# Whole-buffer weight splits, 1024-column loads and row-indexed token DMAs in a two-block transformer forward pass

## The chip, the cores and the metric

The kernel runs on one core of one Trainium2 chip. The metric is device time in microseconds of one execution. Before the change the median of three runs is 2467.13 us (2462.75 to 2468.89).

## What is computed

The input is x, 256 tokens of width 1024 in float32. A first block has two layers of four sequence mixers (their branches gated and merged) and a feed-forward part; that part is dense in layer 0 and a mixture of eight experts, two per token, in layer 1. A second block of two layers (latent attention, pooling, a spatial gate, a convolution, and a feed-forward part) follows. The change concerns the mixture of experts, and the way in which every weight is prepared.

```python
def swiglu(h, w1, w3, w2):
    return (jax.nn.silu(h @ w1) * (h @ w3)) @ w2

def moe_ffn(h, router_w, w1, w3, w2):            # h [1, 256, 1024]; w1, w3 [8, 1024, 2816]; w2 [8, 2816, 1024]
    logits = (h @ router_w).astype(jnp.float32)
    top_vals, top_idx = lax.top_k(logits, TOP_K)  # TOP_K = 2
    top_w = jax.nn.softmax(top_vals, axis=-1)
    gate = jnp.sum(jax.nn.one_hot(top_idx, N_EXPERTS) * top_w[..., None], axis=-2)
    out = jnp.zeros_like(h)
    for e in range(N_EXPERTS):
        out = out + gate[..., e:e + 1] * swiglu(h, w1[e], w3[e], w2[e])
    return out
```

## The kernel before

**Weights.** All weights come from DRAM in float32, in buffers of 128 partitions by 1024 columns (`raw`, and `rawp` for buffers that are halves of a larger tile; six everywhere, twenty in the experts). `wload` (L171) splits each into two parts in TensorE's format `fp32r` whose sum is the weight: ScalarE casts it (L190, `whi`), and VectorE or GpSimd subtracts (L191, `wlo` = `raw` - `whi`). It does so in pieces of at most 512 columns, two a buffer, with ten pairs of piece buffers (`SPBUFS`). Every seventh piece in the experts (`POOLN`), every third elsewhere (`POOLD`), is subtracted on GpSimd. A product of activations and weights is then three TensorE products of 128x512 (`mm3`: high x high at L231, low x high at L232, high x low at L233).

**An expert** (`swiglu`, L1072) works on at most 128 gathered tokens. Its first two weights, w1 and w3, are 1024x2816. They are loaded in buffers of two blocks of 128 rows by 512 columns, so each row that a DMA reads is 2 KB (1 KB for the last 256 columns): 48 buffers. For each 512 columns the two results stand in two banks `mm`; ScalarE applies SiLU, VectorE multiplies (`ffa`), TensorE transposes, and a cast (L238) with a subtraction (L239) makes the pair `G`. The second weight, w2, has 22 buffers of 128 rows by 1024 columns (4 KB a row). `accumulate` sums its products. So an expert has 70 buffers and eight experts have 560.

**Tokens.** `route` (L1115) ranks the logits on VectorE and gives each token a slot in its two experts. `gather` (L1159) builds a one-hot matrix `oh` of 128 slots, fetches the row scale of each slot with a product (L1170), the rows with eight products of `oh` with the split tokens `xs` (L1181), scales them into two halves `ffa` (L1183) and transposes them (L359) into the pair `xgT`. It also transposes `oh` itself (L1188) into `ohT`. It is called between the first and the second weights of the expert before, so that an expert's tokens are ready at its start. After w2, `done` splits the result (`yeh`, `yel`), multiplies it with `ohT` (L1211, L1212, eight products) and adds it, times the gate, onto x (L1214). `xs` itself is made once ahead of the router: two casts on ScalarE (L1224) and two subtractions of 1024 columns on GpSimd (L1225).

**What sets the order.** A scheduler places the instructions of each engine by data, buffers and priorities: weight work (`WPRIO`) behind what the next products wait for (`CPRIO`). Loads are issued by SyncE and start as soon as a `raw` buffer is free; a split waits for a free pair. Within an engine the order is fixed: an instruction that waits holds up all that stand behind it. If an expert got more than 128 tokens, a second pass would run under a condition at the end; with these inputs it doesn't.

Of the kernel before, what the change touches and what calls it, by code (L numbers as in the profile page):

```python
# [15 lines left out]
D = 1024  # L16
S = 256
# [5 lines left out]
KH = 2  # L23


def const_tables():
# [30 lines left out]
    c["iota1"] = np.broadcast_to((i + 1.0)[None, :], (128, 128))  # L57
    inv = np.float32(10000.0) ** (-np.arange(0, 32, 2, dtype=np.float32) / np.float32(32))
# [12 lines left out]
CBASE = ["U", "L", "ones", "before", "iota1"]  # L71
# [52 lines left out]
class Net:  # L124
    def __init__(self, ctx, tc, A, offs):
# [25 lines left out]
        self.nload, self.npiece, self.more, self.pool_every = 0, 0, False, POOLD  # L151
# [3 lines left out]
    # products that only bring TensorE to its full clock, while the first loads are under way  # L155
# [13 lines left out]
    # ---- weights: loaded in float32, split exactly into two float32r parts; w[k][j] is the pair for  # L169
    # the columns j * width .. of the rows k * 128 ..  # L170
    def wload(self, src, width=512, raw=None):  # L171
        nc = self.nc
        srcs = src if isinstance(src, list) else [src]
        k = srcs[0].shape[0] // 128
        n = sum(a.shape[1] for a in srcs)
        out = []
        with self.prio(WPRIO):
            if raw is None:
                raw = self.raw()
                self.wdma(raw, srcs)  # L180
            rv = raw[:, :k * n].rearrange("p (k c) -> p k c", k=k)
            for kk in range(k):
                row = []
                for c in range(0, n, width):
                    m = min(width, n - c)
                    hi = self.wp.tile([128, 512], F32R, tag="whi", name="whi", bufs=SPBUFS)
                    lo = self.wp.tile([128, 512], F32R, tag="wlo", name="wlo", bufs=SPBUFS)
                    self.npiece += 1
                    eng = nc.gpsimd if self.pool_every and self.npiece % self.pool_every == 0 else nc.vector
                    nc.scalar.copy(hi[:, :m], rv[:, kk, c:c + m])  # L190
                    eng.tensor_tensor(lo[:, :m], rv[:, kk, c:c + m], hi[:, :m].bitcast(F32), ALU.subtract)  # L191
                    row.append((hi, lo))
                out.append(row)
# [50 lines left out]
    # mul / sqrt(ss * inv_n + eps): a guess from the exponent bits, then three Newton steps  # L244
    # y <- (y*y*v - c) * y, whose factors -2, -8 and -512 the last step takes out
# [27 lines left out]
    # sums of squares of one half of a row tile  # L273
# [65 lines left out]
    # out = p * r of token tile t ; out = p * r along the tokens  # L339
# [12 lines left out]
    # token-major [128, n*128] -> feature-major split columns of token tile t  # L352
# [67 lines left out]
    # one 2 KB slot (512 columns) viewed as shape  # L420
# [6 lines left out]
    # one such slot for what a product leaves in PSUM  # L427
# [25 lines left out]
    # out = 2 * silu(src) = (1 + tanh(src / 2)) * src  # L453
# [4 lines left out]
    # min(z,0) and log(1 + exp(-|z|))  # L458
# [10 lines left out]
    # silu of the causal convolution; w and b come halved  # L469
# [11 lines left out]
    # rmsnorm of each 64-wide head of o [128, 2, 256] times gate, to feature-major  # L481
# [14 lines left out]
    # token-major y [128, 2, n*128] -> pair [128, n, 256], gains g [128, n]  # L496
# [18 lines left out]
    # ---- first block's branches  # L515
# [316 lines left out]
    # tanh of half the gate of one branch, feature-major: the gate is half of 1 + that  # L832
# [12 lines left out]
    # twice the gated product of a branch, summed into merged [128, 8 * S]; the last one splits the sum  # L845
# [21 lines left out]
    # sum over k of lhs(k, t) x w[k] into banks ps[t][c]; the last rows go tile by tile, so that  # L867
    # what follows one tile runs under the products of the other
# [47 lines left out]
    # done: adds to x; with r, by token  # L916
# [100 lines left out]
    # ---- gated feed-forward: the first 256 features token-major, tile by tile, the others feature-major  # L1017
# [40 lines left out]
    # feature-major product of one 128-row block of the weights with all tokens  # L1058
# [11 lines left out]
    # token-major, for one tile of gathered tokens  # L1070
    def swiglu(self, hT, w1, w3, w2, between, done):
        nc = self.nc  # L1072
        G = [self.T([128, FF // 128, 128], f"G{i}", F32R) for i in range(2)]
        for c0 in range(0, FF, 512):
            n = min(512, FF - c0)
            ps = [self.mm() for m in range(2)]
            for k0 in range(0, KD, KH):
# [80 lines left out]
    def gather(self, e, base, xs, g, sel, pos, rp):  # L1158
# [26 lines left out]
        for c in range(2):  # L1185
            self.to_T([v[:, 4 * c:4 * c + 4] for v in gT], xg[c], 0, 4)
# [504 lines left out]
```

## Time and profile before

| | us |
|---|---|
| median of 3 runs (lowest, highest) | 2467.13 (2462.75, 2468.89) |
| span of the profiled execution | 2465.5 |
| TensorE busy | 2401.7 (97%) |
| VectorE busy | 1861.0 (75%) |
| ScalarE busy | 1580.9 (64%) |
| GpSimd busy | 857.9 (35%) |
| routed experts, 766.8 to 1585.3 | 818.5 |

The profile is one execution, recorded by the hardware. Busy times sum an engine's instructions; TensorE's products overlap in a pipeline, so the distance of their starts is what one costs, not its own duration. A window is a stretch of the span; "granted clock" is the share of TensorE's full clock that it was given there. In a row, `out<-in` are the program's names, `L233` the line of the code, and `[idle before <-releaser]` the idle time ahead of an instruction and what ended it. PE is TensorE, PEld its weight loads, DVE VectorE, ACT ScalarE, POOL GpSimd.

### The profile page before, as it was taken

To read this page: it belongs to the slowest core of one execution; us is meant where nothing else is said; L and a number is where in the kernel's file an instruction comes from. 1 tells how busy PE (TensorE), PEld (TensorE's weight loads), DVE (VectorE), ACT (ScalarE), POOL (GpSimd) and SP (SyncE) were. 2 spreads that over 40 slices of the span, in tenths; PEclk is the share of its full clock that TensorE was granted. 3 is DMA by queue.
4 is the path that set the end of the run, shared out by engine and by line. 5 is a ranking of instruction groups with operands and counts; after the bars stand their busy time and mean duration, and the time that the engine had idled before them with its cause. 6 is when DMAs were issued, how large, how long until landed. Compare 5 with 4: busy or idle time off the path is not lost. (4 is left out here: it accounts for less than half of the span.)

```text
span 2465.5 us, 43800 instructions
## 1 busy us (share of the span) xinstructions
PE 2401.7 (97%) x15094; PEld 2144.3 (87%) x15094; DVE 1861.0 (75%) x3294; ACT 1580.9 (64%) x3026; POOL 857.9 (35%) x631
## 2 busy tenths in 40 slices
PE   9999999999998999999999999899999999999998
PEld 8999899899997787877878887699989979998997
DVE  6887654579868998999989999885575558557554
ACT  7554655566456888888888887665455546545553
POOL 4435333343442333344333243222423223142332
PEclk9999999999998999999999999899999999999999
DMA  7445565644468999998999998564556655455663
GB/s 252 129 145 165 178 186 186 197 145 137 142 201 294 328 327 356 324 348 326 321 357 329 345 341 315 197 188 137 167 159 201 184 177 155 121 164 162 197 182 109
DMA packets 253018, 547.00 MB, mean 222 GB/s; under 512 B 17392, under 2 KB 44272, under 8 KB 252528
## 3 DMA queue, kind: packets, MB, share of 16 engines
q1 hardware_dynamic: 252784, 544.10, 67.1%
q8 instruction: 120, 1.97, 0.3%
q14 instruction: 114, 0.93, 0.1%
HBM read 542.98 MB, written 1.05 MB: 221 GB/s over the span
## 5 line engine op out<-in xcount | busy, mean ns | idle before, releaser
L190 ACT CAST whi<-raw 128x512 fp32r<-128x512 f32 (+1 forms) x1772 | 1040.0, 607 | 574.7 <-PE mm L1064 223.5
L191 DVE TENSOR_TENSOR wlo<-raw,whi 128x512 fp32r<-128x512 f32 (+2 forms) x1331 | 982.8, 770 | 367.2 <-ACT whi L190 346.7
L191 POOL TENSOR_TENSOR wlo<-raw,whi 128x512 fp32r<-128x512 f32 (+1 forms) x441 | 673.7, 1528 | 1377.8 <-ACT whi L190 848.7
L1062 PE MATMUL mm<-hT,whi 128*128 128x256 f32 x1904 | 543.6, 286 | 2.6 <-ACT cin L341 2.6
L1063 PE MATMUL mm<-hT,wlo 128*128 128x256 f32 x1904 | 544.1, 286 | 0.9 <-DVE wlo L191 0.9
L1064 PE MATMUL mm<-hT,whi 128*128 128x256 f32 x1904 | 542.2, 285 | 0.0
L1062 PEld LDWEIGHTS mm<-hT,whi 128*128 128x128 f32 x1904 | 361.9, 190 | 7.2 <-ACT cin L341 2.8
L1063 PEld LDWEIGHTS mm<-hT,wlo 128*128 128x128 f32 x1904 | 361.9, 190 | 5.3 <-issue 2.6
L1064 PEld LDWEIGHTS mm<-hT,whi 128*128 128x128 f32 x1904 | 361.8, 190 | 3.8 <-issue 2.4
L232 PE MATMUL mm<-whi,xgT 128*128 128x512 f32 (+1 forms) x768 | 289.0, 377 | 0.0
L231 PE MATMUL mm<-whi,xgT 128*128 128x512 f32 (+1 forms) x768 | 288.2, 376 | 0.2 <-ACT xgT L238 0.2
L233 PE MATMUL mm<-wlo,xgT 128*128 128x512 f32 (+1 forms) x768 | 286.3, 380 | 0.6 <-DVE wlo L191 0.4
L233 PE MATMUL mm<-wlo,G 128*128 128x512 f32 x616 | 240.6, 402 | 13.7 <-POOL wlo L191 13.3
L231 PE MATMUL mm<-whi,G 128*128 128x512 f32 x616 | 244.3, 397 | 0.0
L232 PE MATMUL mm<-whi,G 128*128 128x512 f32 x616 | 244.2, 396 | 0.0
L191 DVE TENSOR_TENSOR wlo<-rawp,whi 128x512 fp32r<-128x512 f32 (+1 forms) x288 | 209.4, 777 | 5.0 <-ACT whi L190 4.6
L190 ACT CAST whi<-rawp 128x512 fp32r<-128x512 f32 (+1 forms) x336 | 192.5, 601 | 31.9 <-PE mm L232 14.5
L232 PEld LDWEIGHTS mm<-whi,xgT 128*128 128x128 f32 x768 | 144.5, 188 | 29.0 <-DVE xgT L239 0.4
L233 PEld LDWEIGHTS mm<-wlo,xgT 128*128 128x128 f32 x768 | 144.0, 188 | 29.4 <-DVE wlo L191 2.5
L231 PEld LDWEIGHTS mm<-whi,xgT 128*128 128x128 f32 x768 | 144.6, 188 | 27.5 <-ACT xgT L238 0.5
L233 PEld LDWEIGHTS mm<-wlo,G 128*128 128x128 f32 x616 | 117.3, 190 | 42.6 <-POOL wlo L191 16.1
L232 PEld LDWEIGHTS mm<-whi,G 128*128 128x128 f32 x616 | 117.3, 190 | 26.9
(520 smaller groups left out, 3842.6 us busy)
## 6 DMA issues: line engine op xcount, KB each, us to landing
raw<-in_moe_w SPq DMA_DIRECT2D x344, 512.0 KB, 6.3
raw<-in_w_in SPq DMA_DIRECT2D x208, 512.0 KB, 3.7
rawp<-in_moe_w SPq DMA_DIRECT2D x152, 512.0 KB, 6.2
raw<-in_ffn_w SPq DMA_DIRECT2D x62, 512.0 KB, 3.9
raw<-in_w_ffn_down SPq DMA_DIRECT2D x44, 512.0 KB, 3.6
raw<-in_w_ffn_gate SPq DMA_DIRECT2D x40, 512.0 KB, 4.2
raw<-in_w_ffn_up SPq DMA_DIRECT2D x40, 512.0 KB, 4.1
raw<-in_w_out SPq DMA_DIRECT2D x32, 512.0 KB, 4.0
```

Of the source, the lines that this page charges most:

```text
L190: nc.scalar.copy(hi[:, :m], rv[:, kk, c:c + m])
L191: eng.tensor_tensor(lo[:, :m], rv[:, kk, c:c + m], hi[:, :m].bitcast(F32), ALU.subtract)
L231: mm(out, a[0], b[0], start=start, stop=False)
L232: mm(out, a[1], b[0], start=False, stop=False)
L233: mm(out, a[0], b[1], start=False, stop=stop)
L1062: mm(o, wh, xh, start=start, stop=False, skip_group_check=True)
L1063: mm(o, wl, xh, start=False, stop=False, skip_group_check=True)
L1064: mm(o, wh, xl, start=False, stop=stop, skip_group_check=True)
```

## The change

Four things change together.

- **Split.** `wload` splits a whole buffer at a time: one cast of up to 1024 columns on ScalarE, then one subtraction of the first columns on VectorE and one of the rest on GpSimd. VectorE takes 768 of 1024 columns in the experts (`DPARTM`), 704 elsewhere (`DPART`). There are five pairs of whole buffers, the same space as ten halves.
- **First weights.** w1 and w3 are loaded as 128 rows by 1024 columns, 4 KB a row (768 columns, 3 KB, at the end). The four results of 1024 columns stand in two banks `mm` and two banks `sm`. It is again 48 buffers, 32 of 1024 and 16 of 768 columns.
- **Fetch.** The normalised tokens (`h` = x times row scale times gain, two VectorE operations at L1303 in a tile named `yrow`) are stored once to DRAM (`hrows`), by a DMA from ScalarE's queue. For experts 1 to 7 a product of `oh` with the token numbers gives the indices, VectorE casts them (`gidx`), and GpSimd issues an indirect DMA that fetches 128 rows of 4 KB into `xrow`. The first expert is gathered by four products in full float32 on x.
- **Collect.** ScalarE copies the results of experts 0 to 6 from PSUM (`yrow`) and stores them to DRAM (`yrows`); rows beyond an expert's tokens aren't used. Inside expert 7, four indirect DMAs fetch for each token the row of its better and of its second expert, and four VectorE operations add them, times the gates, onto x. A zero row stands in for expert 7, which keeps the old scatter. Some fifteen tiny VectorE operations (`places`) make the indices.

The core of the diff:

```diff
-            rv = raw[:, :k * n].rearrange("p (k c) -> p k c", k=k)
-            for kk in range(k):
-                for c in range(0, n, width):
-                    m = min(width, n - c)
-                    hi = self.wp.tile([128, 512], F32R, tag="whi", name="whi", bufs=SPBUFS)
-                    lo = self.wp.tile([128, 512], F32R, tag="wlo", name="wlo", bufs=SPBUFS)
-                    self.npiece += 1
-                    eng = nc.gpsimd if self.pool_every and self.npiece % self.pool_every == 0 else nc.vector
-                    nc.scalar.copy(hi[:, :m], rv[:, kk, c:c + m])
-                    eng.tensor_tensor(lo[:, :m], rv[:, kk, c:c + m], hi[:, :m].bitcast(F32), ALU.subtract)
+            hi = self.wp.tile([128, RAWCOLS], F32R, tag="whi", name="whi", bufs=SPBUFS)
+            lo = self.wp.tile([128, RAWCOLS], F32R, tag="wlo", name="wlo", bufs=SPBUFS)
+            cut = k * n * self.dve_part // 1024 // 32 * 32
+            nc.scalar.copy(hi[:, :k * n], raw[:, :k * n])
+            for eng, c0, c1 in ((nc.gpsimd, cut, k * n), (nc.vector, 0, cut)):
+                eng.tensor_tensor(lo[:, c0:c1], raw[:, c0:c1], hi[:, c0:c1].bitcast(F32), ALU.subtract)
...
-        for c0 in range(0, FF, 512):
-            ps = [self.mm() for m in range(2)]
-            for k0 in range(0, KD, KH):
-                    wt = self.wload(w[k0 * 128:(k0 + KH) * 128, c0:c0 + n])
+        for c0 in range(0, FF, 1024):
+            cs = [min(512, FF - c) for c in range(c0, min(c0 + 1024, FF), 512)]
+            ps = [[self.mm() for _ in cs], [self.sm() for _ in cs]]
+            for k in range(KD):
+                    wt = self.wload(w[k * 128:(k + 1) * 128, c0:c0 + n])[0]
...
+    def gather_first(self, g, sel, pos, rp):
...
-                for i in range(2):
-                    nc.tensor.matmul(p, P[:, t], xs[t][i][:, cs], start=t + i == 0, stop=t + i == 2)
-            nc.vector.scalar_tensor_tensor(xg[c], p, r, g[:, cs], ALU.mult, ALU.mult)
+                nc.tensor.matmul(p, P[:, t].bitcast(F32), self.x[t][:, cs], start=t == 0, stop=t == 1)
+            nc.vector.scalar_tensor_tensor(xg[:, cs], p, r, g[:, cs], ALU.mult, ALU.mult)
...
+    def gather(self, e, base, sel, pos):
+        P = self.slots(e, base, sel, pos)
+        p = self.sm("pT")
+        for t in range(2):
+            nc.tensor.matmul(p[:, 0:2], P[:, t], self.tokid[:, 2 * t:2 * t + 2], start=t == 0, stop=t == 1)
+        nc.vector.tensor_copy(idx, p[:, 0:1])
+        nc.gpsimd.indirect_dma_start(xg, None, self.hrows, bass.IndirectOffsetOnAxis(ap=idx[:, 0:1], axis=0))
+        for c in range(2):
+            self.to_T([v[:, 4 * c:4 * c + 4] for v in gT], xg[:, c * 512:(c + 1) * 512], 0, 4)
+        return gT, self.slots_T(P) if base or e == NE - 1 else None
...
+        def store(_, c, py):
+            nc.scalar.copy(self.yrow[:, c * 512:(c + 1) * 512], py)
+            if c == 1:
+                nc.scalar.dma_start(self.yrows[e * 128:(e + 1) * 128, :], self.yrow)
...
-                nc.scalar.copy(hi, self.x[t])
-                nc.gpsimd.tensor_tensor(lo, self.x[t], hi.bitcast(F32), ALU.subtract)
...
+            nc.vector.scalar_tensor_tensor(h, self.x[t], self.r[t], g, ALU.mult, ALU.mult)
+            nc.scalar.dma_start(self.hrows[t * 128:(t + 1) * 128, :], h)
...
+        def collect():
+            for t in range(2):
+                for j in range(2):
+                    nc.gpsimd.indirect_dma_start(y, None, self.yrows,
+                                                 bass.IndirectOffsetOnAxis(ap=idx[:, q:q + 1], axis=0))
+                    nc.vector.scalar_tensor_tensor(self.x[t], y, g2[:, t, j:j + 1], self.x[t], ALU.mult, ALU.add)
...
-SPBUFS = 10
+SPBUFS = 5
-POOLN = 7
-POOLD = 3
+DPARTM = 768
+DPART = 704
```

Where instructions stand changes too. On GpSimd, ahead of and in the first expert before, stand the two subtractions `xs` and then single pieces:

```order
L191 TENSOR_TENSOR wlo<-raw,whi 128x512 x11
L1225 TENSOR_TENSOR xs_9241<-x_68,xs_9240 128x1024
L1225 TENSOR_TENSOR xs_9245<-x_69,xs_9244 128x1024
L191 TENSOR_TENSOR wlo<-raw,whi 128x512 x3
L191 TENSOR_TENSOR wlo<-rawp,whi 128x512
L191 TENSOR_TENSOR wlo<-raw,whi 128x512 x4
L191 TENSOR_TENSOR wlo<-rawp,whi 128x512 x2
L191 TENSOR_TENSOR wlo<-raw,whi 128x256
```

In the changed kernel GpSimd has a narrower subtraction for each buffer; this is the stretch in the first expert from the last columns of w1 and w3 (128x192) into w2 (128x256), with the fetch of the second expert's rows behind nine of w2's:

```order
L191 TENSOR_TENSOR wlo<-raw,whi 128x192 x6
L191 TENSOR_TENSOR wlo<-rawp,whi 128x192 x2
L191 TENSOR_TENSOR wlo<-raw,whi 128x256 x8
L191 TENSOR_TENSOR wlo<-rawp,whi 128x256
L1239 DMA xrow<-hrows,gidx 128x1024
L191 TENSOR_TENSOR wlo<-rawp,whi 128x256 x3
L191 TENSOR_TENSOR wlo<-raw,whi 128x256 x6
L191 TENSOR_TENSOR wlo<-rawp,whi 128x256 x2
```

GpSimd's work went from one piece in seven to a part of each buffer, and its queue now also holds DMAs. On TensorE the transposes of the next expert's rows stood, before, among the products of the second weights (`G`):

```order
L231 MATMUL mm<-whi,G_9358 128x512
L232 MATMUL mm<-whi,G_9359 128x512
L359 MATMUL pT<-lead,ffa 128x128 x8
L233 MATMUL mm<-wlo,G_9358 128x512
L231 MATMUL mm<-whi,G_9358 128x512
```

and the scatter of an expert's result stood among the next expert's first products:

```order
L233 MATMUL mm<-wlo,xgT_10215 128x512
L1211 MATMUL sm<-yeh,ohT 128x512 x2
L231 MATMUL mm<-whi,xgT_10215 128x512
L232 MATMUL mm<-whi,xgT_10216 128x512
L1212 MATMUL sm<-yel,ohT 128x512 x2
```

After the change, at the edge between two experts:

```order
L233 MATMUL mm<-whi,G_9702 128x512
L234 MATMUL mm<-whi,G_9703 128x512
L235 MATMUL mm<-wlo,G_9702 128x512 x2
L361 MATMUL pT<-lead,xrow 128x128 x8
L233 MATMUL mm<-whi,xgT_10401 128x512 x2
L233 MATMUL sm<-whi,xgT_10401 128x512 x2
L234 MATMUL mm<-whi,xgT_10402 128x512
L235 MATMUL mm<-wlo,xgT_10401 128x512
```

The transposes moved to the very edge, behind the last product of the second weights, and no scatter follows (line numbers are two higher in the changed code). On VectorE, in the router's chain before, the ranking follows the logits at once:

```order
L321 COPY rr<-rsz 128x2
L322 TENSOR_SCALAR rr<-rsz 128x2
L1124 COPY lg<-sm 128x16
L451 TENSOR_TENSOR lg<-lg,sm 128x16
L239 TENSOR_TENSOR rp<-rr,rp 128x2
L451 TENSOR_TENSOR ffa<-lg 128x128 x2
L1146 TENSOR_REDUCE lmx<-lg 128x2
```

and after the change the two operations that make `h` (in `yrow`) stand between the two:

```order
L323 COPY rr<-rsz 128x2
L324 TENSOR_SCALAR rr<-rsz 128x2
L453 TENSOR_TENSOR lg<-lg,sm 128x16
L1303 SCALAR_TENSOR_TENSOR yrow<-x_68,rr,gain 128x1024
L1303 SCALAR_TENSOR_TENSOR yrow<-x_69,rr,gain 128x1024
L453 TENSOR_TENSOR ffa<-lg 128x128 x2
```

The ranking moved behind two operations of 1024 columns.

## Rows read from the trace of the kernel before

**Rows 1.** The page: the span, and each engine's busy time, share and instructions.

```profile
span 2465.5 us, 43800 instructions
PE 2401.7 (97%) x15094; PEld 2144.3 (87%) x15094; DVE 1861.0 (75%) x3294; ACT 1580.9 (64%) x3026; POOL 857.9 (35%) x631
```

**Rows 2.** Window: length, busy PE, PEld, DVE, ACT, POOL; clock, DMA share, GB/s.

```profile
60.00:440.00 380.00, 379.18 (x2819) 357.04 (x2819) 256.44 (x475) 203.09 (x382) 137.99 (x114) 1.00 0.54 165
```

**Rows 3.** Windows of experts 0 to 4, 5 and 6, 7.

```profile
766.80:1284.00 517.20, 503.91 (x2342) 413.25 (x2343) 482.84 (x721) 439.81 (x790) 192.57 (x99) 0.99 0.93 333
1284.00:1483.60 199.60, 199.60 (x942) 164.06 (x941) 193.89 (x283) 167.26 (x312) 72.20 (x40) 1.00 0.96 342
1483.60:1585.30 101.70, 100.23 (x457) 79.56 (x455) 95.48 (x137) 76.88 (x152) 31.25 (x19) 1.00 0.73 260
```

**Rows 4.** TensorE's waits by releaser: us in total, times, longest.

```profile
PE mm L233 <- POOL wlo L191: 13.3, 5, 2.8
```

**Rows 5.** Timeline of GpSimd in expert 2: start, us, instruction, idle before.

```profile
1035.07 0.78 POOL L191 TENSOR_TENSOR wlo<-rawp,whi 128x256 fp32r<-128x256 f32 x1 [2.88 <-PE mm L233]
...
1053.50 1.38 POOL L191 TENSOR_TENSOR wlo<-raw,whi 128x512 fp32r<-128x512 f32 x1 [3.10 <-PE mm L232]
1059.25 8.64 POOL L191 TENSOR_TENSOR wlo<-raw,whi 128x512 fp32r<-128x512 f32 x1 [4.37 <-PE mm L232]
```

**Rows 6.** Timeline of VectorE beside these three.

```profile
1035.32 0.81 DVE L191 TENSOR_TENSOR wlo<-rawp,whi 128x256 fp32r<-128x256 f32 x1
...
1053.65 1.78 DVE L191 TENSOR_TENSOR wlo<-rawp,whi 128x512 fp32r<-128x512 f32 x1
...
1058.87 4.89 DVE L191 TENSOR_TENSOR wlo<-raw,whi 128x512 fp32r<-128x512 f32 x8
```

**Rows 7.** Groups of VectorE, 860 to 1460 (six experts): busy us, mean ns.

```profile
L451 DVE TENSOR_TENSOR ffa<-mm,ffa 128x512 f32<-128x512 f32 x30 | 20.4, 680 | 0.0
L239 DVE TENSOR_TENSOR G<-pT,G 128x512 fp32r<-128x512 f32 x30 | 20.3, 677 | 0.4 <-ACT G L238 0.4
L1214 DVE SCALAR_TENSOR_TENSOR x<-sm,egate,x 128x512 f32<-128x512 f32 x24 | 17.3, 740 | 2.1 <-PE sm L1212 2.1
...
L1183 DVE SCALAR_TENSOR_TENSOR ffa<-sm,rslot,gain 128x512 f32<-128x512 f32 x12 | 8.4, 745 | 0.5
...
L239 DVE TENSOR_TENSOR G<-pT,G 128x256 fp32r<-128x256 f32 x6 | 2.5, 409 | 0.0
```

**Rows 8.** Timeline of TensorE in expert 4: starts of products that don't wait.

```profile
1228.02 0.40 PE L231 MATMUL mm<-whi,xgT 128*128 128x512 f32 x1
...
1229.41 0.40 PE L231 MATMUL mm<-whi,xgT 128*128 128x512 f32 x1
```

**Rows 9.** The tile xs: durations in ns (min/median/max), first and last start.

```profile
L1224 ACT CAST xs<-x x2: 1048/1052/1056, 747.3 to 749.3; 128x1024 fp32r<-128x1024 f32 x2
L1225 POOL TENSOR_TENSOR xs<-x,xs x2: 2331/2567/2803, 748.9 to 751.7; 128x1024 fp32r<-128x1024 f32 x2
```

**Rows 10.** Windows in expert 0: second weights, then expert 1's first.

```profile
837.00:875.40 38.40, 35.65 (x155) 28.60 (x154) 33.90 (x52) 29.25 (x52) 16.43 (x7) 0.96 0.96 350
875.40:941.00 65.60, 65.60 (x318) 54.42 (x317) 63.07 (x94) 58.55 (x108) 22.86 (x14) 1.00 0.93 332
```

**Rows 11.** Groups of VectorE, 749 to 757, ahead of the router.

```profile
L250 DVE TENSOR_SCALAR rsv<-nss 128x2 f32<-128x2 f32 x1 | 2.3, 2271 | 0.0
...
L451 DVE TENSOR_TENSOR nss<-xss 128x1 f32<-128x1 f32 x1 | 1.7, 1704 | 0.0
...
L256 DVE TENSOR_TENSOR rsu<-rsy 128x2 f32<-128x2 f32 x3 | 0.5, 160 | 0.1
```

**Rows 12.** Groups of ScalarE over the span: the cast of half a buffer.

```profile
L190 ACT CAST whi<-raw 128x512 fp32r<-128x512 f32 x1640 | 987.3, 621 | 557.3 <-PE mm L1064 223.5 <-PE sm L1064 128.0 <-PE mm L232 93.3
```

**Rows 13.** Line 329, a full-float32 product: ns of a record.

```profile
L329 PE MATMUL prb<-dg,cbase x14: 377/378/628, 22.7 to 2286.5; 128*128 128x256 f32 x14
```

**Rows 14.** Timeline of TensorE: the first gather's products for one half.

```profile
761.11 2.05 PE L1181 MATMUL sm<-xs,oh 128*128 128x512 f32 x4
```

More of the change, by code (lines that the diff above doesn't have):

```diff
@@ L23 @@
 KH = 2
+ZROW = 128 * (NE - 1)
 def const_tables():
@@ L68, in const_tables @@
     return {k: np.ascontiguousarray(v.astype(np.float32)) for k, v in c.items()}
-CBASE = ["U", "L", "ones", "before", "iota1"]
+CBASE = ["U", "L", "ones", "before", "iota1", "tokid", "row", "stored"]
 CONE = ["caus", "mneg", "qcos", "qsin", "kcos", "ksin", "swap", "gsub", "gblk", "hmask", "bmask"]
@@ L1167, in gather, with slots_T, gT @@
                                     ALU.is_equal, ALU.mult)
+        return P
+    def slots_T(self, P):
+        pP = self.sm("pT")
+        for t in range(2):
+            self.nc.tensor.transpose(pP[:, t * 128:t * 128 + 128], P[:, t].bitcast(F32), self.ident)
+        PT = self.T([128, S], "ohT", F32R)
+        self.nc.scalar.copy(PT, pP[:, :S])
+        return PT
+    def gT(self):
+        return [self.T([128, KD, 128], f"xgT{i}", F32R) for i in range(2)]
+    def gather_first(self, g, sel, pos, rp):
+        nc = self.nc
+        P = self.slots(0, 0, sel, pos)
         pP = self.sm("pT")
@@ L1189, in gather @@
-        PT = self.T([128, S], "ohT", F32R, bufs=2)
-        nc.scalar.copy(PT, pP[:, :S])
-        return gT, PT
-    def experts(self, base, gate, *a, first=None):
-        gathered = first or self.gather(0, base, *a)
+                nc.tensor.matmul(p, P[:, t].bitcast(F32), self.x[t][:, cs], start=t == 0, stop=t == 1)
+            nc.vector.scalar_tensor_tensor(xg[:, cs], p, r, g[:, cs], ALU.mult, ALU.mult)
+            self.to_T([v[:, 4 * c:4 * c + 4] for v in gT], xg[:, cs], 0, 4)
+        return gT, None
@@ L1195, in experts, with between @@
+    def experts(self, base, gate, sel, pos, first, before_last):
+        gathered = first or self.gather(0, base, sel, pos)
         for e in range(NE):
             ahead = []
-            self.expert(e, gathered, gate,
-                        lambda: ahead.append(self.gather(e + 1, base, *a) if e + 1 < NE else None))
-            gathered = ahead[0]
+            def between():
+                if e + 1 < NE:
+                    ahead.append(self.gather(e + 1, base, sel, pos))
+                elif before_last:
+                    before_last()
+            self.expert(e, gathered, gate, between)
+            gathered = ahead and ahead[0]
@@ L1214, in done @@
                 nc.vector.scalar_tensor_tensor(xs, p, gate[:, t, e:e + 1], xs, ALU.mult, ALU.add)
-        self.swiglu(gT, A["moe_w1"][0, e], A["moe_w3"][0, e], A["moe_w2"][0, e], between, done)
+        self.swiglu(gT, A["moe_w1"][0, e], A["moe_w3"][0, e], A["moe_w2"][0, e], between, store if PT is None else add)
     def moe(self, l):
         nc, tc = self.nc, self.tc
-        xs = []
-        with self.prio(0):
-            for t in range(2):
-                hi, lo = [self.T([128, D], f"xs{i}", F32R, bufs=2) for i in range(2)]
-                nc.scalar.copy(hi, self.x[t])
-                nc.gpsimd.tensor_tensor(lo, self.x[t], hi.bitcast(F32), ALU.subtract)
-                xs.append((hi, lo))
@@ L1227, in moe @@
-        with self.prio(CPRIO):
-            sel, gate, pos, rp = self.route(self.hT)
-            g = self.gain(self.A["ffn_norm_g"][l])
-            a = (gate, xs, g, sel, pos, rp)
-            first = self.gather(0, 0, *a[1:])
-        self.pool_every, self.more = POOLN, True
-        self.experts(0, *a, first=first)
-        self.pool_every, self.more = POOLD, False
+        with tc.tile_pool(name="rows", bufs=1, space=bass.MemoryType.DRAM) as rows:
+            self.hrows = rows.tile([S, D], F32, name="hrows")
+            self.yrows = rows.tile([ZROW + 1, D], F32, name="yrows")
+            self.moe_in(l)
```

101 lines of the change are left out of this document (71 added, 30 removed).

## The prediction

> **What bounds the kernel now.** The page comes first: TensorE is busy for 97% of the profiled span of 2465.5 us, VectorE for 75% [rows 1]. A share near 100% says little where stages differ, so the windows come second. From 60 to 440 us TensorE is busy 379.18 of 380.00 us while VectorE has 256.44 [rows 2]: outside the routed experts TensorE alone decides. The experts run from 766.8 to 1585.3 us, 818.5 us for eight. There VectorE is nearly as full as TensorE [rows 3]: experts 5 and 6 take 199.60 us together, 99.8 each, TensorE without a gap, VectorE 193.89, which is 96.9 an expert or 97%. Experts 0 to 4 take 517.20, 103.4 each. The excess is 517.2 - 5 x 99.8 = 18.2 us. The waits name its start: five times TensorE waited for a low part that GpSimd made, 13.3 us in all [rows 4]; the rest goes with the restart, at a mean granted clock of .99 against 1.00.
>
> The timelines say why GpSimd is late. Its 512-column subtraction that begins at 1059.25 lasts 8.64 us, the one before it 1.38 [rows 5]; in that time VectorE runs eight of its own back to back from 1058.87, 4.89 us, .61 each [rows 6]. The other way round, VectorE's at 1053.65 took 1.78 while GpSimd ran the one of 1053.50, and its 256-column one at 1035.32 took .81 under GpSimd's of 1035.07. The two engines exclude each other in these subtractions. So GpSimd's piece costs VectorE time: 1.78 - .68 = 1.10 us for 512 columns, .81 - .41 = .40 for 256 (.68 and .41 are VectorE's lone times for these sizes, [rows 7]).
>
> **The split, per expert.** Before: 140 pieces, 124 of 512 columns and 16 of 256; every seventh, 20, on GpSimd. VectorE: about 106 x .61 + 14 x .34 = 69.5 us. Its other work by [rows 7] (five ffa and five G at .68, one of each at .41, the yel and xgT pairs at .68, four x sums at .74, two gathered halves at .745, small ones 1.2) is 16.0, so 85.5. GpSimd's holds: 17.7 x 1.10 + 2.3 x .40 = 20.4. In series that is 105.9, while VectorE shows 96.9 busy. Since it idles only 2.9 an expert, the holds are really about (96.9 + 2.9 - 85.5) / 20.4 = .70 of my price or less.
>
> After: 70 buffers, 54 of 1024 columns and 16 of 768. VectorE takes three quarters. The step from 256 to 512 columns is .27, so 768 columns are .61 + .27 = .88 and 576 are .68: 54 x .88 + 16 x .68 = 58.4. The other work loses gathered halves, sums and yel: 9.6. Together 68.0 against 85.5. GpSimd now has a part of every buffer, 54 of 256 and 16 of 192 columns. Price of a hold between .40 and .55 (half of 1.10); I take .55 and .41: 36.3. So GpSimd's share of holds grows by 16 while VectorE's own work falls by 17.5: in series 104.3 against 105.9, at the .70 above 68.0 + 25.4 = 93.4 against 99.8. The whole-buffer split hardly changes the sum; it changes that no buffer does without GpSimd.
>
> [...] Rows 5 and 6 agree that one blocks the other; they show less than the whole instruction as the price. What full length would make of the time is a rival below.
>
> ScalarE casts a whole buffer in 1.05 us [rows 9] instead of twice .62 [rows 12]. It was busy 167.26 of 199.60 us [rows 3] and becomes less so; I cost it at nothing here.
>
> **TensorE, per expert.** Products cost .232 us each: 1.39 us for six from 1228.02 to 1229.41 [rows 8]. The eight gather products, eight of the same size for the scatter, and the slots' transposes and row scales (.3) go: 16 x .232 + .3 = 4.0. So 99.8 - 4.0 = 95.8. Against that stands the order. The eight transposes of the next expert's rows stood inside the second product, under cover; now they stand after its last buffer, directly ahead of products that need their result, through two casts and two subtractions. Nothing covers that: about a cast (.62, [rows 12]) and a subtraction (.68), less a little overlap, 1.2 us. So TensorE needs 97.0.
>
> **The transfers.** 34.6 MB an expert. In the stretch of 4 KB rows (the second weights) they ran at 350 GB/s with a share of .96, in that of 2 KB rows at 332 with .93 [rows 10]: 365 against 357 at full share, 2% for the longer rows. With 1 MB more for rows stored and fetched, 35.6 MB / 365 = 97.5 us an expert. Three needs, 93.4, 97.0 and 97.5, lie close; before they were at most 99.8, 99.8 and 95.8 (.96 of 99.8, [rows 3]), and experts came to 99.8 or, where GpSimd was starved, 103.4. I take **99 us**: 1.5 above the largest need, for what is left of waits on GpSimd (before, the mean of 102.3 stood 2.5 above it). GpSimd can now hold up any buffer, with five split buffers ahead as before (ten halves). 8 x 99 = 792.0 against 818.5: **-26.5**.
>
> **The indirect DMAs.** GpSimd issues one fetch per expert (seven) and four collects; in its queue three to nine splits of an expert's second weights stand ahead, the others behind. VectorE casts the indices, which waits for a small product; GpSimd's fetch waits for the cast; behind both stand splits that TensorE waits for. ScalarE's new stores wait only for its own copies. The trace has no such DMA. Bounds of what one takes of GpSimd: 0, and 8.64 as the starved subtraction [rows 5], which with four to five buffers ahead costs what a starvation cost, 18.2 / 5 = 3.6 us. A gain is excluded: GpSimd does nothing less. Nearest are its 1024-column operations, 2.33 and 2.80 us [rows 9]: less than the four buffers ahead last (4 x 99 / 70 = 5.7), so I take 0 on the path. The fetch is issued some 80 products, 19 us, before the transposes.
>
> **Edges.** The start: GpSimd's two subtractions xs (2.33, 2.80) held up two tiny operations of the norm that the router waits for, to 1.70 and 2.27 us against .16 for others of their size [rows 11]; they go, -3.6. In their place two 1024-column operations of VectorE (h) stand between the logits and the ranking: .74 + .54 = 1.28 each, +2.6. The first gather's products become full float32. Such a product of 256 columns shows up as two records of .38 us [rows 13], against one for the others, and the old eight took 2 x 2.05 = 4.1 us at the lower clock there [rows 14]; half as many of more passes: +3 (0 to 4). The end: expert 7 keeps the eight scatter products and the slots' transposes (+2.2), and four collected sums add 4 x 1.28 = 5.1 on VectorE, half of it taken as hidden by the expert's products (+2.5). Sum -3.6 + 2.6 + 3 + 2.2 + 2.5 = 6.7, **+7** (0 to 12).
>
> **Elsewhere.** TensorE is the bound [rows 2] and VectorE and GpSimd have room. What is uncovered is the first buffer of a phase: it waits for a whole cast (1.05) where half (.62) did, +.43, some dozen times: **+5** (0 to 12).
>
> **Sum:** -26.5 + 7 + 5 = -14.5; 2465.5 - 14.5 = 2451.0. The median of the runs (2467.1) lies 1.6 above the profiled span: 2452.6, **2453**.
>
> **Rivals.** (a) *Nothing waits.* With 97 an expert: 776 - 818.5 + 12 = -30.5, so **2437**. For it: experts 5 and 6 reach their bound exactly. Against it: five of eight don't. (b) *The exclusion is served in series (slower).* Each buffer needs both engines, and VectorE's run of .88 for GpSimd's every .55: with no overlap 104.3 an expert, 834.4, so +15.9 + 12 = +27.9: **2495**. It decides from an expert of 100.8 on ((818.5 - 12) / 8). For it: the 8.64 us row, and that GpSimd had 20 pieces an expert and now has 70. Against it: before, the same sum was 105.9 and 99.8 was reached. (c) *The whole instruction is held,* at .78 for 256 columns and, by the step of .60 to 1.38 for 512 [rows 5], .63 for 192: 68.0 + 42.1 + 10.1 = 120.2 an expert, 961.6, +143 + 12: **2622**. Against it: before, the same prices give 85.5 + 17.7 x 1.38 + 2.3 x .78 = 111.7 where 99.8 was reached. [...] (d) *Fetches block GpSimd:* 7 x 3.6 = +25 on the forecast, **2478**. For it: nothing in the trace excludes it. [...]
>
> **How the numbers follow.** Forecast .45, (a) .17, (b) .20, (c) .03, (d) .15. Predicted 2453. The range of 8 in 10 runs from below (a), 2430, to past (b), 2500: out lie (c), under half of (b) and the tails below (a), some .2. A measurement of this kernel tells .3%, 7.4 us, from no change: 2459.7 to 2474.5 counts as the same. Forecast: .36 faster, .06 same, .03 slower; (a) .17 faster; (b) .03 same, .17 slower; (c) .03 slower; (d) .06 same, .09 slower, since 7.4 us of its price are open either way. Sums .53, .15, .32.
>
> **What would show it.** In the profile after: experts of 99 us in the windows, VectorE below 97% of them, TensorE's waits on GpSimd's low parts under 2 us each expert; a gap near 1.2 us before each expert's first product; the fetch landing well before its transposes; a share of the transfers near .98. It is wrong if experts exceed 100.8, if GpSimd's operations of 256 columns last several us in a row, or if the waits on GpSimd begin at the fetch.

## The result, and the profile after

The changed kernel takes 2495.36 us (median of four runs, 2492.6 to 2498.41) against 2466.02: **1.2% slower**, ratio 1.0121 with a 95% interval of 1.0107 to 1.0135. The prediction said 2453, range 2430 to 2500. The time lies inside the range, on the wrong side of no change, and next to the number of rival (b). That number is met by accident, as the sums below show.

The page after, to be read against [rows 1]:

```profile
span 2495.2 us, 42205 instructions
PE 2399.9 (96%) x14968; PEld 2115.2 (85%) x14968; DVE 1836.6 (74%) x2693; ACT 1398.5 (56%) x1950; POOL 1519.4 (61%) x1207
```

TensorE's busy time hardly moved although some 27 us of products are gone by the prediction's count, so busy time here is more than work; what else it holds was not taken apart. GpSimd went from 35% to 61%.

Windows after (length, busy time by engine, granted clock, DMA share, GB/s): experts 0 to 6, then expert 7 with its end, against [rows 3].

```profile
779.60:1489.10 709.50, 687.93 (x3172) 541.45 (x3170) 670.12 (x605) 523.02 (x600) 618.56 (x493) 1.00 0.94 347
1489.10:1607.60 118.50, 104.80 (x450) 79.00 (x450) 105.87 (x93) 72.62 (x85) 82.63 (x73) 0.97 0.67 242
```

An expert takes 101.4 instead of the 102.4 of before (first seven), where 99 was forecast, and expert 7 takes 118.5. TensorE's waits after, against [rows 4] (us, times, longest):

```profile
PE mm L235 <- DVE wlo L191: 14.4, 14, 3.1
PE mm L233 <- ACT hT L308: 9.4, 4, 3.2
PE mm L234 <- DVE hT L311: 6.2, 4, 3.7
PE pT L1092 <- DVE ffa L453: 5.6, 10, 1.3
PE sm L235 <- DVE wlo L191: 5.3, 6, 2.1
...
PE mm L233 <- ACT xgT L240: 4.6, 4, 2.4
```

Of the waits on GpSimd two short ones are left (1.4 us, in expert 7); in their place stand many on VectorE's part of the split, on the norms (`hT`, outside the experts) and at the experts' edges (`xgT`). By stage, from the two profiled executions, in us:

| stage | before | after | change | forecast |
|---|---|---|---|---|
| outside (norm to norm, without the experts' stage) | 1617.4 | 1635.1 | +17.7 | +5 |
| from the norm to the first expert | 23.5 | 28.6 | +5.1 | +2 |
| experts 0 to 6 | 716.8 | 709.5 | -7.3 | -23.8 |
| expert 7 to the next norm | 107.9 | 122.0 | +14.1 | +2 |

**Where the experts' time goes** is seen in two timelines. In expert 1 the two engines alternate (start, us, instruction):

```profile
957.87 4.33 DVE L191 TENSOR_TENSOR wlo<-raw,whi 128x768 fp32r<-128x768 f32 x3
```

```profile
957.09 5.70 POOL L191 TENSOR_TENSOR wlo<-raw,whi 128x256 fp32r<-128x256 f32 x4
```

That is about 1.42 us a buffer on either (5.70 for four of GpSimd's, 4.33 for three of VectorE's): .88, the prediction's price of VectorE's part, and .54 for GpSimd's, as if each engine were shut out while the other works. In expert 7, GpSimd makes one split in .74 us, most of it before VectorE's next begins at 1518.37, issues two collects and has seven splits to make up:

```profile
1517.81 0.74 POOL L191 TENSOR_TENSOR wlo<-raw,whi 128x256 fp32r<-128x256 f32 x1
1518.70 1.50 POOL L1313 DMA_INDIRECT xrow<-yrows,pidx  x1
1520.50 1.41 POOL L1313 DMA_INDIRECT xrow<-yrows,pidx  x1 [0.30 <-PE sm L235]
1521.93 3.50 POOL L191 TENSOR_TENSOR wlo<-raw,whi 128x256 fp32r<-128x256 f32 x5
1525.40 1.39 POOL L191 TENSOR_TENSOR wlo<-rawp,whi 128x256 fp32r<-128x256 f32 x2
```

and VectorE beside it:

```profile
1518.37 3.60 DVE L191 TENSOR_TENSOR wlo<-raw,whi 128x768 fp32r<-128x768 f32 x4
...
1521.89 5.71 DVE L191 TENSOR_TENSOR wlo<-raw,whi 128x768 fp32r<-128x768 f32 x1
```

Beside the DMAs VectorE takes .90 a buffer (3.60 for four), near the .88 of its price; beside GpSimd's seven subtractions without a pause one of VectorE's lasts 5.71 us. It is the 8.64 us row of [rows 5] with the engines exchanged: in both rows the one that has a queue keeps the other out.

### The profile page after: what moved, and what is told of

Read it like the earlier page. It is cut to its first block, busy times and chain, and to the rows that moved or that the text cites. A ratio compares the mean times of both kernels' runs of the same rounds, so it can differ in the third digit from the quotient of the medians.

```text
span 2495.2 us, 42205 instructions
## 1 busy us (share of the span) xinstructions
PE 2399.9 (96%) x14968; PEld 2115.2 (85%) x14968; DVE 1836.6 (74%) x2693; ACT 1398.5 (56%) x1950; POOL 1519.4 (61%) x1207
## 5 line engine op out<-in xcount | busy, mean ns | idle before, releaser
L191 POOL TENSOR_TENSOR wlo<-raw,whi 128x320 fp32r<-128x320 f32 (+2 forms) x886 | 1194.5, 1362 | 847.9 <-ACT whi L189 746.6
L191 DVE TENSOR_TENSOR wlo<-raw,whi 128x704 fp32r<-128x704 f32 (+2 forms) x886 | 979.0, 1131 | 447.7 <-ACT whi L189 438.7
L189 ACT CAST whi<-raw 128x1024 fp32r<-128x1024 f32 (+1 forms) x886 | 891.6, 1026 | 632.6 <-PE mm L1066 156.9
L191 POOL TENSOR_TENSOR wlo<-rawp,whi 128x256 fp32r<-128x256 f32 (+1 forms) x168 | 205.2, 1239 | 42.1 <-ACT whi L189 36.6
L235 PE MATMUL mm<-wlo,G 128*128 128x512 f32 x616 | 221.4, 400 | 5.2 <-DVE wlo L191 4.8
L191 DVE TENSOR_TENSOR wlo<-rawp,whi 128x768 fp32r<-128x768 f32 (+1 forms) x168 | 209.8, 1290 | 4.7 <-ACT whi L189 3.8
L189 ACT CAST whi<-rawp 128x1024 fp32r<-128x1024 f32 (+1 forms) x168 | 165.6, 1002 | 49.2 <-PE mm L234 25.2
L233 PE MATMUL mm<-whi,xgT 128*128 128x512 f32 (+1 forms) x384 | 146.8, 384 | 7.8 <-ACT xgT L240 4.6
L234 PE MATMUL mm<-whi,xgT 128*128 128x512 f32 (+1 forms) x384 | 143.4, 380 | 3.4 <-DVE xgT L241 3.4
L233 PE MATMUL sm<-whi,xgT 128*128 128x512 f32 (+1 forms) x384 | 145.6, 380 | 0.6 <-ACT whi L189 0.6
L234 PE MATMUL sm<-whi,xgT 128*128 128x512 f32 (+1 forms) x384 | 142.4, 377 | 0.0
L234 PEld LDWEIGHTS mm<-whi,G 128*128 128x128 f32 x616 | 116.1, 188 | 25.8
L233 PEld LDWEIGHTS mm<-whi,G 128*128 128x128 f32 x616 | 116.2, 189 | 25.1 <-ACT whi L189 1.1
```

The source lines that it names most:

```text
L189: nc.scalar.copy(hi[:, :k * n], raw[:, :k * n])
L191: eng.tensor_tensor(lo[:, c0:c1], raw[:, c0:c1], hi[:, c0:c1].bitcast(F32), ALU.subtract)
L233: mm(out, a[0], b[0], start=start, stop=False)
L234: mm(out, a[1], b[0], start=False, stop=False)
L235: mm(out, a[0], b[1], start=False, stop=stop)
```

## The experiments

All times are medians beside runs of before on the same chip (2464 to 2467 us).

**GpSimd's share in the experts.** First no share:

```diff
-DPARTM = 768
+DPARTM = 1024
```

> The changed kernel, except that in the experts VectorE subtracts the whole buffer and GpSimd none of it (outside the experts as changed). Theory 'exclusion': the two engines' subtractions shut each other out, and TensorE, which needs 95.5 us an expert, waits for that. VectorE alone needs 54 x 1.15 + 16 x .88 + 9.6 = 86 us an expert, so experts 1 to 6 fall from a mean of 102.1 to about 97, expert 7 from 118.5 to about 101, and the time to about 2450. Rival 'transfers and edges': the longer rows, the row traffic or the transposes at the edge set the pace of the experts; then they stay at 101 to 102 and the time at 2485 or more.

2460.12 us, ratio to before .9984 (.9970 to .9998), 35 less than changed. Then more and less than the changed kernel's 256 columns (640 and 896 in the same line):

> The changed kernel with VectorE's part in the experts at 640 of 1024 columns instead of 768 (GpSimd 384). Theory 'in series': a buffer costs the sum of both engines' parts, .88 + .54 = 1.42 us now and .75 + .82 = 1.57 then, so an expert grows by some 9 us and the time to about 2565. Rival 'side by side': VectorE's part gets shorter, GpSimd's 1.02 us are still below TensorE's 1.37 a buffer, and the time stays below 2510.

2577.03 us.

> The changed kernel with VectorE's part in the experts at 896 of 1024 columns (GpSimd 128). Theory 'in series': a buffer costs 1.01 + .27 = 1.28 us, below TensorE's 1.37, so the engines catch up after a wait: experts 3 to 6 fall from 102.3 to about 99, expert 7 by some 5, the time to about 2475. Rival 'side by side': no change, 2490 or more.

2477.25 us. The windows of experts 0 to 6 (of 640: 0 to 5), for VectorE's 1024, 896 and 640 columns:

```profile
780.40:1470.70 690.30, 681.20 (x3172) 552.82 (x3170) 595.26 (x603) 521.99 (x600) 10.74 (x7) 1.00 0.94 356
```

```profile
778.40:1474.00 695.60, 682.67 (x3172) 551.71 (x3170) 613.21 (x604) 521.56 (x598) 524.40 (x492) 1.00 0.94 354
```

```profile
776.50:1443.40 666.90, 620.65 (x2718) 479.40 (x2716) 612.95 (x519) 448.71 (x512) 584.79 (x421) 0.97 0.89 317
```

With GpSimd at 0, 128, 256 and 384 columns an expert takes 98.6, 99.4, 101.4 and 111.2 us, while the two parts in series cost, by the prices above (estimates from [rows 5] to [rows 7]; 1.42 is also measured), 1.15, 1.28, 1.42 and 1.57 us for a buffer of 1024 columns, for which TensorE needs six products, 6 x .232 = 1.39 [rows 8]. The bend lies where the sum passes TensorE's need. "Side by side" is out: VectorE's part is smallest at 640 columns, where the time is worst.

**The indirect DMAs.** Without the collect (x lacks the results of seven experts):

```diff
-        self.experts(0, gate, sel, pos, first, collect)
+        self.experts(0, gate, sel, pos, first, None)
```

> The changed kernel without the collect: no indirect DMAs from the stored results and no sums of them onto x (so x lacks the results of experts 0 to 6). Theory 'backlog': in expert 7 the collects put GpSimd behind, its backlog of subtractions then shuts VectorE out; without them expert 7 falls from 118.5 to about 104 and the time to about 2481. Rival 'the last expert is long for its own scatter and end': expert 7 stays above 113, the time above 2489.

2482.33 us. Expert 7 to the next norm falls from 122.0 to 108.4. Without the fetch (wrong tokens' rows):

```diff
-        nc.gpsimd.indirect_dma_start(xg, None, self.hrows, ...)
+        nc.sync.dma_start(xg, self.hrows[0:128, :])
```

> The changed kernel, but each expert's rows come by an ordinary DMA of the first 128 stored rows from SyncE's queue, so GpSimd issues no fetch (the rows are the wrong tokens' for all experts but the first). If the fetches cost nothing on the path, as the prediction had it, the time stays within 4 us of 2495. If each costs what a starvation cost before (3.6 us), it falls by 25 to about 2470.

2483.17 us: between the two theories. Expert 2 gives back 8.7 us (105.2 to 96.5), the others up to 1.7 each. But this run changes more than who issues the fetch. The plain DMA waits for no indices, so the rows come earlier (the seventh is issued at 1249.2, in the changed kernel at 1458.8), and the transposes stand again among the products `G`, as in the kernel before, and not at the open edge:

```profile
L1239 SPq DMA_DIRECT2D xrow<-hrows x7: 326/382/384, 786.3 to 1249.2; - x7
```

```profile
1143.42 0.65 PE L361 MATMUL pT<-lead,xrow 128*128 128x128 f32 x4
1143.83 0.70 PE L235 MATMUL mm<-wlo,G 128*128 128x512 f32 x2
```

TensorE's waits in experts 0 to 6 tell the two apart. In the changed kernel they are

```profile
PE mm L233 <- ACT xgT L240: 4.2, 3, 2.4
PE mm L234 <- DVE xgT L241: 3.4, 2, 3.0
...
PE mm L235 <- DVE wlo L191: 2.5, 7, 0.7
PE sm L235 <- DVE wlo L191: 1.7, 4, 0.4
```

and with the plain DMA

```profile
PE mm L235 <- DVE wlo L191: 2.4, 5, 1.0
...
PE sm L235 <- DVE wlo L191: 1.7, 4, 0.4
```

The waits on the splits are the same, 4.2 and 4.1 us; those on the transposed rows, 7.6 us, are gone. The longest stood at expert 2's edge in the changed kernel. VectorE, which takes 1.42 us a buffer beside GpSimd (5.69 for four), has four splits ahead of the subtraction of the rows, and TensorE waits for that one:

```profile
973.46 5.69 DVE L191 TENSOR_TENSOR wlo<-raw,whi 128x768 fp32r<-128x768 f32 x4
979.07 1.27 DVE L241 TENSOR_TENSOR xgT<-pT,xgT 128x512 fp32r<-128x512 f32 x2
```

```profile
979.80 0.79 PE L234 MATMUL mm<-whi,xgT 128*128 128x512 f32 x1 [2.99 <-DVE xgT L241]
```

From 975.6 to 985.0 the granted clock is .64 on the mean, from 985.0 to 1080.8 it is 1.00. So most of the 12 us is the open edge and not GpSimd's issue. Without both:

> The changed kernel with neither kind of indirect DMA: rows by an ordinary DMA (the wrong tokens) and no collect (x lacks seven experts). The two alone gave 12 and 13 us. If GpSimd's issue of them is a loss of its own at each place, the sum shows: about 2470. If both only tip the same balance, less: 2478 or more. What stays above before (2465) is then the five whole buffers outside the experts (15 us), less what the experts gain.

2468.86 us, ratio 1.0014 (1.0000 to 1.0028): the losses add up, 13 + 12 against 26.5, as they lie in different experts. Experts 0 to 6 take 697.5 us (709.5 in the changed kernel), expert 7 to the next norm 108.9 (122.0). Here too the transposes have left the edge, so the sum doesn't show that the issue costs at each place. What GpSimd spends on the DMAs is small:

```profile
L1239 POOL DMA_INDIRECT xrow<-hrows,gidx x7: 954/957/1427, 854.7 to 1458.8; - x7
```

About 1 us for a fetch and 1.0 to 1.9 for a collect, but 3.3 us of time for each collect. Two engines that together need 1.42 us for a buffer that costs TensorE 1.39 have nothing to make up a loss with (argued from these two rates), and what GpSimd makes up it takes from VectorE, as the row of 5.71 us shows. The other runs bear it out. With the collects in it, expert 7 to the next norm takes 122.0 us where GpSimd has 256 columns, 116.2 at 128 and 107.8 at none; without them it takes 108.4 at 256. The run without the collect lacks VectorE's four sums too, but the run with VectorE alone has them and takes no longer.

**The stages outside.** Pieces of 512 columns outside the experts, in the five whole buffers:

```diff
+                for c0 in ...:                       # 512 columns at a time, every third on GpSimd
+                    nc.scalar.copy(hi[:, c0:c1], raw[:, c0:c1])
+                    eng.tensor_tensor(lo[:, c0:c1], raw[:, c0:c1], hi[:, c0:c1].bitcast(F32), ALU.subtract)
```

> The changed kernel, but outside the experts weights are split in pieces of 512 columns as before, every third on GpSimd (in the experts as changed). Theory 'grain': the 17.8 us by which the stages outside the experts grew come from whole-buffer casts and subtractions that stand ahead of what the norms wait for; they go, and the time falls to about 2477 with experts unchanged. Rival: they come from other things that moved (banks, order); then it falls by 5 or less, to 2490 or more.

2493.1 us: "grain" falls, at least as a matter of the instructions' size. Then the split of before with its ten half buffers, loads and token DMAs as changed:

```diff
-            hi = self.wp.tile([128, RAWCOLS], F32R, tag="whi", name="whi", bufs=SPBUFS)   # 5
+                    hi = self.wp.tile([128, 512], F32R, tag="whi", name="whi", bufs=SPBUFS)   # 10
```

> The changed kernel with the split of before everywhere: 512-column pieces in ten pairs of half buffers, every seventh on GpSimd in the experts, every third elsewhere; loads of 1024 columns and the token DMAs stay. Theory 'lock step and lumps': the whole-buffer split makes both losses, the experts' alternation of the two engines and, outside, buffers that come free in lumps of 1024 columns. Then the stages outside take what they took before (17 us less), experts 1 to 6 about 98.5, and the time is about 2446. Rival 'the outside grew for another reason': it stays 14 to 17 us long there, and the time is about 2460.

2487.55 us: half right. Outside, the stages are back at 1615.1 us, so the buffers' size makes that loss (the profiles with whole buffers have 1625.3 to 1635.1 us there, those with half buffers 1611.5 to 1617.4); but the experts got longer, 103.8 on average. Over its span TensorE's products into `mm` waited twice for a low part of GpSimd's, 5.0 us, 2.9 the longest (2.8 in [rows 4]), and 22 times for one of VectorE's, 16.4 us. And the whole-buffer split alone on the kernel before:

> The kernel before with the whole-buffer split alone (768 of 1024 columns on VectorE in the experts, 704 elsewhere, five pairs of buffers); loads in 512 columns, one-hot gather and scatter stay. Theory: in series the two engines need 74.4 + 36.3 = 110.7 us an expert, of which an expert takes about 107, and the stages outside grow by 14: about 2517. Rival 'the tokens' DMAs made the loss': within 10 us of before, at most 2476.

2462.41 us, ratio .9995 (.9983 to 1.0007). My 2517 was far off. Outside it loses 15 us; the experts gain 20, for TensorE has no gap in seven of them:

```profile
775.40:1471.80 696.40, 696.40 (x3283) 573.30 (x3283) 679.21 (x654) 533.74 (x613) 538.44 (x487) 1.00 0.96 345
```

99.5 an expert: with gather and scatter TensorE needs 99.5 / 70 = 1.42 us a buffer on the mean of all its work, against 95.5 / 70 = 1.36 in the changed kernel, so the two engines have more time. The split is no loss in the experts by itself; it holds them up where TensorE needs less. There it does so even without the indirect DMAs: experts 3 to 6 take 405.7 us with neither kind, 408.3 in the changed kernel, and 397.8 with VectorE alone.

How the buffers lengthen a norm shows on ScalarE. With pieces in whole buffers (2493.1 us) the casts of the next weights come between the norm's parts, and the cast `hT` that TensorE waits for begins at 2292.50, 4.3 us after its transposes at 2288.22:

```profile
2285.48 2.19 ACT L200 CAST whi<-raw 128x512 fp32r<-128x512 f32 x4 [3.25 <-issue]
2287.57 0.63 ACT L288 ACTIVATE junk<-x 128x512 f32<-128x512 f32 x1
...
2288.20 1.12 ACT L200 CAST whi<-raw 128x512 fp32r<-128x512 f32 x2
...
2289.85 2.16 ACT L200 CAST whi<-raw 128x512 fp32r<-128x512 f32 x4
...
2292.50 1.88 ACT L318 ACTIVATE hT<-pT,lead 128x128 fp32r<-128x128 f32 x7
```

With half buffers all ten casts are done before the norm begins:

```profile
2280.43 6.67 ACT L196 CAST whi<-raw 128x512 fp32r<-128x512 f32 x10
2288.73 0.63 ACT L282 ACTIVATE junk<-x 128x512 f32<-128x512 f32 x1 [1.63 <-DVE x L1552]
...
2289.36 1.12 ACT L312 ACTIVATE hT<-pT,lead 128x128 fp32r<-128x128 f32 x4
```

A whole buffer comes free only with the last product that reads either half, which at a stage's end is when the norm starts; that reading of the order is argued, the two orders of ScalarE are shown.

**The loads.** The first weights in 512 columns as before:

```diff
-        for c0 in range(0, FF, 1024):
+        for c0 in range(0, FF, 512):
```

> The changed kernel with the experts' first weights loaded as before, 256 rows by 512 columns; whole-buffer split and token DMAs stay. Theory 'drained reserve': with 1024 columns at a time ScalarE stands before two SiLUs for up to 4.8 us at the end of each stretch of columns (36 us in three experts) and makes no casts, and the two subtracting engines can't catch up. With 512 columns these waits fall below 10 us in three experts, experts 3 to 6 from 102.3 to about 99.5, the time to about 2483. Rival 'the loads don't matter': 2491 or more.

2492.07 us: the loads matter little, as the rival had it.

**Versions without GpSimd in the experts' splits.** The kernel before with one number changed (`POOLN = 0`):

> The kernel before, except that in the experts every piece is on VectorE. VectorE then needs 124 x .61 + 16 x .34 + 16.0 = 97.1 us an expert, TensorE 99.5. Theory: the five starvations of GpSimd go, experts 0 to 4 fall from 103.4 to 99.8, the time by 18 to about 2448. Rival 'VectorE at 97% is itself late': experts at 102 or more, no gain.

2441.00 us, ratio .9904 (.9887 to .9920): better than before and than the change. With loads and token DMAs as changed and the old split:

> As the run with the old split, but in the experts every piece is on VectorE, none on GpSimd. VectorE needs 124 x .61 + 16 x .34 + 9.6 = 90.7 us of the 95.5 that TensorE needs. Theory: no subtraction waits for the other engine, experts 1 to 6 take 97.5, expert 7 about 101, and the time is about 2440. Rival 'VectorE is too full alone': experts stay at 99 or more, and the time is above 2450.

2438.10 us. With the old loads too:

> The kernel before with the token DMAs alone, and in the experts every piece on VectorE (512-column split and loads of before). Against the same with loads of 1024 columns (2438): if longer rows help, experts are bound by transfers, 35.6 MB at 357 GB/s, 99.7 us, and the time is about 2445; if ScalarE's waits at the end of 1024 columns cost something even here, about 2434. Against before with VectorE alone (2441): the token DMAs take 4 us an expert from TensorE's work, of which the uncovered transposes give 2.3 back.

2442.41 us. So the token DMAs and longer rows gain 3 us at most here, although TensorE has 4 us an expert less to do. What eats it was the last open question:

```diff
+            fetched = self.gather(e + 1, base, sel, pos) if e + 1 < NE else None    # at the expert's start
             def between():
-                    ahead.append(self.gather(e + 1, base, sel, pos))
+                    ahead.append(self.gather_T(e + 1, base, fetched))               # transposes only
```

> The kernel with the old split, every piece of the experts on VectorE (2438 us), and each fetch issued one expert earlier, so that the transposes of its rows stand again among the products of the second weights. Theory 'open edge': the wait for the transposed rows, 1.0 to 2.3 us at each of seven edges, is what keeps an expert above TensorE's 95.5; it goes, experts 3 to 6 fall from 99 to about 96.5, the time to about 2424. Rival 'transfers': 35.6 MB an expert at 365 GB/s take 97.5 to 98.5 whatever the edge does; the time falls by 5 at most, to 2433 or more.

2431.97 us, ratio .9868 (.9841 to .9894), the best of all. The edge waits are gone; before that (at 2438.1) one looked like this on TensorE,

```profile
1157.82 0.60 PE L365 MATMUL pT<-lead,xrow 128*128 128x128 f32 x4
1160.55 0.73 PE L237 MATMUL mm<-whi,xgT 128*128 128x512 f32 x2 [2.13 <-ACT xgT L244]
```

and on ScalarE, where the transposed rows' cast stands behind the store's copies and two casts of weights:

```profile
1157.35 1.07 ACT L1270 COPY yrow<-mm 128x512 f32<-128x512 f32 x2 [5.16 <-PE mm L239]
...
1158.87 1.14 ACT L196 CAST whi<-raw 128x512 fp32r<-128x512 f32 x2 [0.45 <-ACT yrow L1270]
1159.92 1.06 ACT L244 CAST xgT<-pT 128x512 fp32r<-128x512 f32 x2
```

Experts 3 to 6 went from 396.6 to 391.3 us, 97.8 each:

```profile
1057.30:1448.60 391.30, 390.04 (x1809) 313.57 (x1808) 353.26 (x621) 313.62 (x626) 47.04 (x3) 1.00 0.96 363
```

The 2.3 us above TensorE's 95.5 remain; whether they are the transfers (363 GB/s at a share of .96) was not tried. TensorE is busy for 390.04 of the 391.30 us, so the 95.5 may itself be too low. In the changed kernel the same edit:

> The changed kernel with each fetch issued one expert earlier and nothing else. If the open edge costs it what the trace shows there (1.0, 1.5, 5.7, 1.4, .7, .7, .5 and the lower clock behind), it falls by about 12 to 2483. If the two subtracting engines in series set the pace of the experts, what the edge gives back is waited for later in the expert, and it falls by under 6.

2487.53 us, 8 less, between the two: experts 1 and 2 fall to 96.8 and 99.0, experts 4 and 5 grow to 105.4 and 103.9. GpSimd still issues every fetch here, so some 8 of the plain DMA's 12 us come back with the edge closed alone. But the fetches now stand elsewhere in GpSimd's queue, and TensorE's waits on VectorE's splits in experts 0 to 6 rise from 4.2 to 10.3 us. What GpSimd's issue of a fetch costs by itself stays open.

## Why the prediction was wrong, point by point

The span is 44 us above the forecast's 2451. By the table of stages 16.5 of them lie in experts 0 to 6, 12 at expert 7, 13 outside and 3 at the router.

- **The indirect DMAs: this step failed.** It took "0 on the path", since one lasts less than the four buffers ahead. The DMA's length was in its bounds (.95 to 1.9 us). What was wrong, as argued above, is the cover: buffers ahead help only if the engines behind are faster than TensorE and refill them, and my own prices had the pair at 1.42 us for a buffer of 1024 columns against TensorE's 1.39. The runs show the loss at the collects: 13 us in expert 7 to the next norm, which took 14.1 more than before where +2 was forecast. Rival (d) had the mechanism but the wrong place: it priced the fetches, at 25, and left out the collects. The fetches' 12 us are mostly the next point.
- **The uncovered edge: mis-sized, and hidden.** The step took 1.2 us and put it inside TensorE's need of 97.0, under the 97.5 of the transfers. TensorE waited 1.8 us on the mean, 2.1 at most, at six edges with the old split on VectorE alone, and 1.30 + 2.99 at expert 2's in the changed kernel: the copies and casts ahead of it on ScalarE were not counted, nor the splits ahead of it on VectorE. And it comes on top. With the edge closed by the plain DMA experts 0 to 6 took 698.2 us, 99.7 each and near the 99 of the forecast, and with it open 709.5.
- **The split.** Its prices held: .88 + .54 shows as 1.42 in the alternation, and the series of 640, 768, 896 and 1024 columns follows it. The conclusion "hardly changes the sum" was right by itself, as the whole-buffer split alone on before shows (experts without a gap). The sum for after, 93.4 against TensorE's 97.0, was too kind: at 256 columns the exclusion costs 101.4 - 98.6 = 2.8 us an expert against VectorE alone, part of it at the edges; without the indirect DMAs it is (405.7 - 397.8) / 4 = 2.0 in experts 3 to 6.
- **Rival (b)** gave 2495 for 104.3 an expert in full series. The experts took 101.4, the rest came from outside and from expert 7; its mechanism acts, its sum met the time by chance. Rival (c) is refuted by the 1.42 us: a hold costs 1.42 - .88 = .54 us of a GpSimd instruction that takes .74 mostly without one of VectorE's splits beside it (the row at 1517.81). The alternation agrees with an exclusion, the .54 not with one of the whole length.
- **Elsewhere:** +5 forecast, +17.7 in the profile, 15 in the whole split alone on before. The step priced a longer first cast; the runs show that the cast's length does next to nothing (pieces: 2493.1) and the size of the buffers that come free nearly all (half buffers: back to 1615.1).
- **TensorE's need** of 95.8 an expert was about right (95.5, by the starts of its products; the best version reaches 97.8 with TensorE almost never idle).
- **The router's edge:** +2 forecast, +5.1 measured; 25 to 26 with half buffers or with the whole split alone, 28 to 30 with whole buffers and token DMAs together. No run took it apart further.
- **The transfers** don't show as a limit in the changed kernel (a share of .94 over experts 0 to 6, where expert 1 reached .97), and the row length, taken as 2%, is worth 4 us at most (2442.4 against 2438.1).

## What to carry to other kernels

Before work is given to an idle engine, ask whether it shuts out the engine it is to relieve: here the best of the shares tried for GpSimd in this stage was none, and one number (`POOLN = 0`) gave 23 us, most of what the whole change lost (29). A pipeline whose helpers have no rate to spare turns each short interruption into lost time (here 1.0 to 1.9 us of GpSimd into 3.3 of the whole for each collect), so price a new instruction on a helper by the rate behind it, not by the buffers ahead. A run that takes an instruction away can also move others, as the plain DMA moved the transposes: read the order before giving the instruction the whole difference. Buffers joined into larger ones seem to free their space later; the loss stood where stages end and norms begin, and not in their middle (from 60 to 440 us TensorE was busy 378.99 of 380 us, 379.18 before).

## What was not expected of the hardware

- The starvation goes both ways: 8.64 us of a GpSimd operation under VectorE's queue [rows 5], 5.71 us of a VectorE one under GpSimd's.
- Issuing two indirect DMAs didn't shut VectorE out: four splits took 3.60 us beside issues of 1.50 and 1.41. From issue to landing a fetch of 128 rows of 4 KB took 5.6 to 8.0 us.
- Two of VectorE's operations with an operand in PSUM let GpSimd run: two `ffa` products of 512 columns (from `sm`) took 1.29 us together, .64 each (.68 for one on the mean of experts 0 to 6), while GpSimd made three splits of 192 columns in 2.06, .69 each. No run shows whether the operand in PSUM is the cause.

```profile
1541.58 1.29 DVE L453 TENSOR_TENSOR ffa<-sm,ffa 128x512 f32<-128x512 f32 x2 [3.76 <-PE sm L235]
```

```profile
1541.31 2.06 POOL L191 TENSOR_TENSOR wlo<-raw,whi 128x192 fp32r<-128x192 f32 x3 [4.09 <-DMA raw<-in_moe_w]
```
